# Preparing the first gated pairs late in layer A's attention, gate weights in half tiles, and output stores issued by ScalarE

## The chip, the cores and the metric

The kernel runs on one core of one Trainium2 chip. The metric is the device time of one execution in microseconds (us). TensorE is called PE here (PEld its weight loads), VectorE DVE, ScalarE ACT, GpSimd POOL, and SyncE, which in the kernel before issues all the DMAs, SP.

## The reference

A decoder trunk of two layers over 2048 tokens of width 1024. Layer A, the one that the change is in, is attention with a forget gate, 16 heads of 64, followed by a gate and an output projection:

```python
u = rmsnorm(h, norm_a_g[i])
q, k, v, f_logit, gate = jnp.split(u @ w_in_a[i], ...)
q, k = rmsnorm(q, qnorm_a_g[i]), rmsnorm(k, knorm_a_g[i])      # per head
log_f = jax.nn.log_sigmoid(f_logit + b_forget[i])
o = fox_attention(q, k, v, log_f)      # causal softmax(q k / 8 + c_q - c_k) v, c = cumsum(log_f)
h = h + (o * jax.nn.silu(gate)) @ w_out_a[i]
```

Layer B computes one shared K/V from the result, then attends in a window of 128 with a sink per head, gates and projects likewise. All in float32.

## The kernel before, in words

Layer A's attention is written as one loop, `for n, (u, p) in enumerate(steps)` (L1116). A unit `u` is a head and a chunk of 512 queries (64 units); a step is one pair of key blocks of a unit, 20 steps per head, 320 in all. A step takes about 2.7 us on the chip, from about 598 to 1474 us of the span.

In a step, `scores` multiplies keys by queries into score banks of PSUM (L975, L976, the mask L979; the tag "sc" has three places), ACT takes the exponential (L984; in a unit's last step L988) and rounds it to a high part (L989), POOL subtracts to get the low part (L990), and DVE adds the exponential to the running sum (L1001). `values` multiplies values by both parts three steps later (L1016); in a unit's last step it copies the result (L1024, ACT) and stores its halves to DRAM as `om` and `oc` (L1026, L1027, SP). Ahead of the scores, `max_pieces` computes row maxima for later units: products on PE (L927), a masked maximum on DVE (L938, L943), with one PSUM place "mx" between them, so that PE's next piece waits until DVE has read the one before.

Into the gaps goes the filler `gate()`: 768 products of the gate projection (L1050), twelve per weight tile of 512 KB (L1046, two places of the tag "wr"), 24 per output tile. When a tile is full, DVE scales it (L1057), ACT applies Tanh (L1058), DVE completes the SiLU (L1059), and SP stores it as `gt` (L1060). 720 of the products are fed in the loop, 48 remain for after it, the last two tiles.

After the loop comes `out_a`, the output projection (product L1219). Its left operand comes in "pairs" of 128 rows by 512 tokens (class `Pairs`, object `op`). A pair is loaded by `gated_load` (om L1167, oc L1168, gt L1169, and rd, the reciprocal sums, in two halves L1172) and prepared by `gated`: om + oc (L1182, POOL), times rd (L1183, DVE), times gt (L1184, DVE), rounded (L1185, ACT), low part (L1186, DVE). `PREP_AT = (284, 298)` loads and prepares pairs 0 and 1 inside the loop at these steps; pair 2 is loaded after it. The output weights of `out_a` are loaded by L122 and split by L131 (ACT) and L132 (DVE).

Python's order is not the chip's: a scheduler orders the instructions of each engine by its own costs, so what is written at step 284 may stand earlier on an engine. Each engine, SP too, then runs its instructions strictly in that order. A tile tag has a fixed number of places (`SLOTS`, L58); a new tile waits until all reads of the one whose place it takes are done.

Of the kernel before, what the change touches and what calls it, by code (L numbers as in the profile page):

```python
# [4 lines left out]

# [1 line left out]

# [15 lines left out]
P = 128  # L23
# [18 lines left out]
SUM_LAG = 5  # L42
LOAD_AT = 7

PREP_AT = (284, 298)

RAW_AT = 302

# [48 lines left out]
class Pairs:  # L97
# [6 lines left out]
        self.loaded = self.ready = 0  # L104

    def load(self, s, tags=("wh", "wl", "wh", "wl")):
        self.tiles[s] = [self.t.sb(tag, [P, CH]) for tag in tags]
        self.t.gated_load(s // NDT, s % NDT, self.tiles[s])
        self.loaded = s + 1

    def prepare(self, s):
        if s % 4 == 0:
            self.Y[s // 4] = self.t.sb("big", [P, 4, 2, CH], F32R)
        self.t.gated(self.y(s), self.tiles.pop(s))
        self.ready = s + 1

    def y(self, s):
# [28 lines left out]
class Trunk:  # L146
# [693 lines left out]
    def attention_a(self, op):  # L840
# [165 lines left out]
        def values(item):  # L1006
            u, p, ph, pl = item
            h, ch = units[u]
            v = heads[h][4]
            if p == 0:  # L1010
                state[u][1] = self.ps("pa", [P, CH])
            pv = state[u][1]
            last = p == 2 * ch + 1
            for n_, (k, q0, w, off) in enumerate(blocks(ch, p)):
                for i, src in enumerate((ph, pl)):
                    nc.tensor.matmul(  # L1016
                        pv[:, q0 : q0 + w], v[:, k, :], src[:, off : off + w],
                        start=(p == 0 and n_ == 0 and i == 0),
                        stop=(last and n_ == 1 and i == 1),
                    )  # L1020
            if last:
                state.pop(u)
                ov = self.sb("sq", [P, CH])
                nc.scalar.copy(ov, pv)  # L1024
                rows, cols = slice(h * HD, (h + 1) * HD), slice(ch * CH, (ch + 1) * CH)
                nc.sync.dma_start(out=d["om"][rows, cols], in_=ov[:HD, :])  # L1026
                nc.sync.dma_start(out=d["oc"][rows, cols], in_=ov[HD:, :])  # L1027

        def gate():


            for ch in range(NCH):
                rows, us = self.factor_rows(0, ch), []
                for dt in range(NDT):
                    us.append([self.sb(t, [P, CH], F32R) for t in ("wh", "wl")])
                    for k in range(2):
                        nc.sync.dma_start(out=f_(us[dt][k]), in_=d["ut"][ch, k, dt])
                for ft in range(NDT):
                    if gate_bank == "mx":
                        ps = self.ps("mx", [P, 2, CH])[:, 0]  # L1040
                    else:
                        ps = self.ps(gate_bank, [P, CH])
                    for dt in range(NDT):
                        if dt % 4 == 0:
                            w = self.sb(next(weight_slots), [P, 2, 2, 2, P], F32R)
                            nc.sync.dma_start(  # L1046
                                out=f_(w), in_=d["wg"][ft, :, dt // 2 : dt // 2 + 2]
                            )
                        for i, (wk, uk) in enumerate(((0, 0), (0, 1), (1, 0))):
                            nc.tensor.matmul(  # L1050
                                ps, w[:, dt // 2 % 2, wk, dt % 2, :], us[dt][uk],
                                start=(dt == 0 and i == 0), stop=(dt == NDT - 1 and i == 2),
                            )
                            if dt < NDT - 1 or i < 2:
                                yield
                    g = self.sb("sq", [P, CH])
                    nc.vector.tensor_tensor(g, ps, rows, ALU.mult)  # L1057
                    nc.scalar.activation(g, g, AF.Tanh, scale=0.5)  # L1058
                    nc.vector.scalar_tensor_tensor(g, g, 1.0, ps, ALU.add, ALU.mult)  # L1059
                    nc.sync.dma_start(  # L1060
                        out=d["gt"][ft * P : (ft + 1) * P, ch * CH : (ch + 1) * CH], in_=g
                    )
                    yield

        pieces, done, loaded = [], 0, 0

# [28 lines left out]
        yield  # L1095
        pht, plt = self.sb("big", [P, 4, 1024], F32R), self.sb("big", [P, 4, 1024], F32R)
        filler, fed, total = gate(), 0, NCH * NDT * NDT * 3
        gate_bank, weight_slots, rest = "pb", cycle(["wr"]), False

        def feed(n, pause=False):  # L1100

# [14 lines left out]
        for n, (u, p) in enumerate(steps):  # L1116
# [17 lines left out]
            if n == RAW_AT:  # L1134
                raw = self.sb("big", [P, NDT // 2, D])
                for p in range(NDT // 2):
                    op.weight_load(p, raw[:, p])
            if n in PREP_AT:
                op.load(PREP_AT.index(n), ("qn", "wh", "qn", "wl"))
                op.prepare(PREP_AT.index(n))  # L1140
        op.load(2, ("qn", "wh", "qn", "wl"))
        gate_bank, weight_slots = "mx", cycle(["st", "wr"])
        for item in pending:
            values(item)
            feed(fed + NDT)
# [2 lines left out]
            recips(*args)  # L1148
        for p in range(PAIRS_READY):
            op.weight_split(p)  # L1150
        for _ in filler:
            pass

# [20 lines left out]
                in_=d["rd"][h : h + 1, cols].to_broadcast([HD, CH]),  # L1174
            )

    def gated(self, y, tiles):

        nc = self.nc
        m, c, g, rb = tiles  # L1180
        yh, yl = (y[:, k] for k in range(2))
        nc.gpsimd.tensor_tensor(m, m, c, ALU.add)  # L1182
        nc.vector.tensor_tensor(m, m, rb, ALU.mult)  # L1183
        nc.vector.tensor_tensor(m, m, g, ALU.mult)  # L1184
        nc.scalar.copy(yh, m)  # L1185
# [350 lines left out]
```

## Time and profile before

| | us |
|---|---|
| median of 3 runs (lowest, highest) | 2511.03 (2509.34, 2516.57) |
| the profiled execution | 2511.7 |
| its span | 2509.9 |
| PE busy in the span | 2462.7 (98%) |
| DVE busy | 1760.2 (70%) |
| ACT busy | 1345.7 (54%) |
| POOL busy | 940.3 (37%) |

The shares are means over stages with different limits. Layer A's attention is the stretch from about 596 to 1494 us; PE is busy almost without a break in it. To read the profile for this change one goes to that stretch, looks at what PE waited for, and then at the timelines of the engines that PE waited for.

### The profile page before, as it was taken

What the parts mean: (1) busy time and instruction counts of PE and PEld (TensorE: products, weight loads), DVE (VectorE), ACT (ScalarE), POOL (GpSimd) and SP (SyncE); (2) the same over time, 40 slices, a digit from 0 to 9 for tenths busy, and PEclk for the clock granted to TensorE, in tenths of its full rate; (3) what the DMA queues carried; (4) which work ended last, traced back from release to release, by engine and by line L of the source; (5) the groups of instructions that cost most, each with busy time, mean ns of one, the idle gap of its engine ahead of it and who ended that gap; (6) DMA issues with size and microseconds to landing.
All of it is one profiled execution on the core that took longest, in us unless ns stands there. A gap on an engine that the chain in (4) does not pass through costs nothing. (4 is left out here: it accounts for less than half of the span.)

```text
span 2509.9 us, 37394 instructions
## 1 busy us (share of the span) xinstructions
PE 2462.7 (98%) x12320; PEld 2054.1 (82%) x12320; DVE 1760.2 (70%) x4255; ACT 1345.7 (54%) x2574; POOL 940.3 (37%) x611
## 2 busy tenths in 40 slices
PE   8999999999999999999999999999999999899999
PEld 6788899988878878877877778888888888688887
DVE  7656666736888888888888865556666323788885
ACT  5423333415777777877777651145332214777774
POOL 0000000014777777777777752200011000455542
PEclk9999999999999999999999999999999999999999
DMA  5656655787555745465475459955443424755551
GB/s 184 201 158 190 178 148 149 204 263 224 138 153 138 210 136 160 139 198 158 121 206 159 145 173 296 283 209 162 115 132 84 137 94 141 205 166 158 160 144 64
DMA packets 351521, 419.31 MB, mean 167 GB/s; under 512 B 64928, under 2 KB 248256, under 8 KB 345152
## 3 DMA queue, kind: packets, MB, share of 16 engines
q1 hardware_dynamic: 351328, 416.92, 56.7%
q8 instruction: 98, 1.61, 0.3%
q14 instruction: 95, 0.78, 0.1%
HBM read 265.29 MB, written 151.40 MB: 166 GB/s over the span
## 5 line engine op out<-in xcount | busy, mean ns | idle before, releaser
L750 PE MATMUL b<-wh,big 128*128 128x512 f32 (+3 forms) x2560 | 769.9, 375 | 9.4 <-ACT wh L480 9.3
L990 POOL TENSOR_TENSOR big<-st,big 128x1024 fp32r<-128x1024 f32 (+1 forms) x320 | 678.6, 2132 | 263.6 <-ACT big L989 181.2
L750 PEld LDWEIGHTS b<-wh,big 128*128 128x128 f32 x2560 | 471.4, 188 | 79.7 <-ACT wh L480 11.2
L750 PE MATMUL b<-wl,big 128*128 128x512 f32 (+3 forms) x1280 | 473.6, 370 | 1.2 <-DVE wl L481 1.2
L1001 DVE TENSOR_TENSOR ac<-ac,st 128x512 f32<-128x512 f32 (+3 forms) x576 | 354.7, 616 | 60.8 <-ACT ac L993 20.7
L984 ACT ACTIVATE st<-sc 128x512 f32<-128x512 f32 (+1 forms) x512 | 275.7, 585 | 130.6 <-PE sc L976 76.0
L1016 PE MATMUL pa<-big 128*128 128x512 f32 (+2 forms) x1280 | 332.5, 373 | 2.1 <-POOL big L990 1.2
L989 ACT CAST big<-st 128x1024 fp32r<-128x1024 f32 (+1 forms) x320 | 302.2, 945 | 7.8
L750 PEld LDWEIGHTS b<-wl,big 128*128 128x128 f32 x1280 | 241.4, 189 | 37.7 <-DVE wl L481 5.3
L1016 PEld LDWEIGHTS pa<-big 128*128 128x128 f32 x1280 | 224.5, 190 | 42.3 <-ACT sq L1024 8.1
L975 PE MATMUL sc<-big 128*128 128x512 f32 (+2 forms) x640 | 246.5, 385 | 1.3 <-DVE st L536 1.0
L938 DVE CUSTOM_DVE_ANT_0 mx<-mx,rot 128x128 f32<-128x128 f32 (+3 forms) x240 | 210.8, 878 | 48.0 <-PE mx L927 45.8
L489 ACT ACTIVATE sq<-b,r 128x512 f32<-128x512 f32 (+2 forms) x128 | 77.8, 608 | 302.8 <-PE b L750 299.8
L976 PE MATMUL sc<-big 67*128 67x512 f32 (+2 forms) x640 | 236.2, 369 | 0.0
L927 PE MATMUL mx<-big 66*128 66x128 f32 (+3 forms) x660 | 189.2, 360 | 6.3 <-DVE mt L938 3.2
L1050 PE MATMUL pb<-wh,wr 128*128 128x512 f32 x488 | 179.7, 399 | 6.3 <-DMA wr<-wg 6.0
L491 DVE TENSOR_REDUCE sm<-sq 128x8 f32<-128x512 f32 (+2 forms) x128 | 74.9, 585 | 139.5 <-ACT sq L489 139.3
L1307 POOL TENSOR_TENSOR st<-st,rs 128x1024 f32<-128x1024 f32 (+1 forms) x64 | 118.4, 1850 | 110.3 <-DVE rs L1306 102.1
L715 PE MATMUL b<-big,wh 128*128 128x512 f32 x512 | 158.5, 391 | 0.5 <-DVE st L721 0.5
L850 POOL MEMSET rot<- 128x1024 bf16 x1 | 1.0, 952 | 421.2 <-PE pb L343 421.2
L927 PEld LDWEIGHTS mx<-big 66*128 66x128 f32 x660 | 116.0, 192 | 35.6 <-DVE mt L938 8.3
L975 PEld LDWEIGHTS sc<-big 128*128 128x128 f32 x640 | 122.9, 192 | 21.6 <-ACT st L984 1.7
(251 smaller groups left out, 4348.3 us busy)
## 6 DMA issues: line engine op xcount, KB each, us to landing
wr<-wg SPq DMA_DIRECT2D x62, 512.0 KB, 4.7
va<-st SPq DMA_DIRECT2D x32, 512.0 KB, 4.6
ka<-st SPq DMA_DIRECT2D x64, 256.0 KB, 3.9
ut<-big SPq DMA_DIRECT2D x16, 1024.0 KB, 5.7
big<-ka SPq DMA_DIRECT2D x16, 1024.0 KB, 4.9
big<-qa SPq DMA_DIRECT2D x16, 1024.0 KB, 5.8
qb<-st SPq DMA_DIRECT2D x64, 256.0 KB, 3.9
big<-qb SPq DMA_DIRECT2D x16, 1024.0 KB, 7.7
```

Of the source, the lines that this page charges most:

```text
L715: nc.tensor.matmul(ps, W[k][dt][:, ft * P : (ft + 1) * P], u[ch][:, dt, :], start=(dt == 0 and i == 0), stop=(dt == NDT - 1 and i == 2),)
L750: nc.tensor.matmul(ps[:, :n], u[tb // 4][:, dt, us], W[k][dt], start=(dt == 0 and i == 0), stop=(dt == NDT - 1 and i == 2),)
L927: mm = nc.tensor.matmul(ps[:, b, :wb], qb[:66, i * P : (i + 1) * P], kb[:66, k0 + b * wb : k0 + (b + 1) * wb], start=True, stop=True,)
L938: nc.vector.tensor_tensor_reduce(out=lg, in0=lg, in1=mask, scale=1.0, scalar=NEG, op0=ALU.add, op1=ALU.max, accum_out=f_(o),)
L975: nc.tensor.matmul(o, ka[:, ks], qa[:, qs], start=not (last and n_), stop=False)
L976: nc.tensor.matmul(o, kb[:, ks], qb[:, qs], start=False, stop=not diag)
L984: nc.scalar.activation(pf[:, off : off + w], ps[:, :w], AF.Exp, scale=HD**-0.5)
L989: nc.scalar.copy(ph[:, :tw], pf[:, :tw])
L990: nc.gpsimd.tensor_tensor(pl[:, :tw], pf[:, :tw], f_(ph[:, :tw]), ALU.subtract)
L1001: nc.vector.tensor_tensor(a_, a_, pf[:, off : off + w], ALU.add)
L1016: nc.tensor.matmul(pv[:, q0 : q0 + w], v[:, k, :], src[:, off : off + w], start=(p == 0 and n_ == 0 and i == 0), stop=(last and n_ == 1 an ...
L1050: nc.tensor.matmul(ps, w[:, dt // 2 % 2, wk, dt % 2, :], us[dt][uk], start=(dt == 0 and i == 0), stop=(dt == NDT - 1 and i == 2),)
```

## The change

It has three parts. The core of the diff:

```diff
-PREP_AT = (284, 298)
+PAIR_AT = (298, 309)
 class Pairs:
     def load(self, s, tags=("wh", "wl", "wh", "wl")):
-        self.tiles[s] = [self.t.sb(tag, [P, CH]) for tag in tags]
+        if len(tags) == 4:
+            self.tiles[s] = [self.t.sb(tag, [P, CH]) for tag in tags]
+        else:
+            both = [self.t.sb(tag, [P, 2, CH]) for tag in tags]
+            self.tiles[s] = [t[:, k] for t in both for k in range(2)]
...
-    def prepare(self, s):
+    def prepare(self, s, adder=None):
...
-        self.t.gated(self.y(s), self.tiles.pop(s))
+        self.t.gated(self.y(s), self.tiles.pop(s), adder or self.t.nc.gpsimd)
...
-                nc.sync.dma_start(out=d["om"][rows, cols], in_=ov[:HD, :])
-                nc.sync.dma_start(out=d["oc"][rows, cols], in_=ov[HD:, :])
+                nc.scalar.dma_start(out=d["om"][rows, cols], in_=ov[:HD, :])
+                nc.scalar.dma_start(out=d["oc"][rows, cols], in_=ov[HD:, :])
...
-                        if dt % 4 == 0:
-                            w = self.sb(next(weight_slots), [P, 2, 2, 2, P], F32R)
-                            nc.sync.dma_start(
-                                out=f_(w), in_=d["wg"][ft, :, dt // 2 : dt // 2 + 2]
-                            )
+                        if dt % 2 == 0:
+                            w = next(weight_slots)
+                            nc.sync.dma_start(out=f_(w), in_=d["wg"][ft, :, dt // 2])
...
+        def weight_halves(*tags):
+            tiles = [self.sb(t, [P, 2, 2, 2, P], F32R) for t in tags for _ in range(2)]
+            return cycle([t[:, k] for t in tiles for k in range(2)])
...
-        gate_bank, weight_slots, rest = "pb", cycle(["wr"]), False
+        gate_bank, weight_slots, rest = "pb", weight_halves("wr"), False
...
-            if n in PREP_AT:
-                op.load(PREP_AT.index(n), ("qn", "wh", "qn", "wl"))
-                op.prepare(PREP_AT.index(n))
+            if n == PAIR_AT[0]:
+                op.load(0, ("qn", "wh", "qn", "wl"))
+            if n == PAIR_AT[1]:
+                op.prepare(0, nc.vector)
+        gate_bank, weight_slots = "mx", cycle(
+            list(islice(weight_halves("st"), 4)) + list(islice(weight_slots, 4))
+        )
+        op.load(1, ("st", "st"))
         op.load(2, ("qn", "wh", "qn", "wl"))
-        gate_bank, weight_slots = "mx", cycle(["st", "wr"])
...
             op.weight_split(p)
+        op.prepare(1, nc.vector)
         for _ in filler:
             pass
...
-        nc.gpsimd.tensor_tensor(m, m, c, ALU.add)
+        adder.tensor_tensor(m, m, c, ALU.add)
```

Pair 0 is written later in the loop and its addition goes to DVE; pair 1 goes behind the loop, with two places of the tag "st" instead of four others, its addition on DVE too. A gate weight tile of twelve products is loaded as two of six, into four places instead of two. The stores of a unit's output are issued by ACT. In the changed kernel the lines are numbered anew: the pair's addition is L1195, its products L1196 and L1197, its low part L1199, its loads L1180 (om), L1181 (oc), L1182 (gt), L1185 (rd); the gate tile's finish L1060 to L1062 and its store L1063, gate weights L1051, maxima L943 and L948, the sums L1006, the output weights' load and split L127, L136 and L137.

The first place is DVE's order between the last maxima (`m`, `mt`) and the running sums (`ac`), where a pair's products (`qn`) stand. Before, pair 0's two products (L1183, L1184):

```order
L938 ISA mx,mt<-mx,rot 128x2x288
L938 ISA mt 128x1
L1001 TENSOR_TENSOR ac<-ac,st 128x512
L1183 TENSOR_TENSOR qn<-qn,wl 128x512
L1001 TENSOR_TENSOR ac<-ac,st 128x512
L943 TENSOR_REDUCE mt<-mx 128x1
L1001 TENSOR_TENSOR ac<-ac,st 128x512
L1184 TENSOR_TENSOR qn<-qn 128x512
```

Now, pair 0's second product (L1197; its first stands four rows above it) and behind it the first product of pair 2 (L1196), which has the same places of "qn":

```order
L1197 TENSOR_TENSOR qn<-qn 128x512
L1006 TENSOR_TENSOR ac<-ac,st 128x512
L943 ISA mx,m<-mx,rot 128x2x384
L943 ISA m 128x1
L1006 TENSOR_TENSOR ac<-ac,st 128x512
L1006 TENSOR_TENSOR ac<-ac,st 128x384
L943 ISA mx,m<-mx,rot 128x2x448
L943 ISA m 128x1
L1006 TENSOR_TENSOR ac<-ac,st 128x256
L1196 TENSOR_TENSOR qn<-qn,wl 128x512
L1006 TENSOR_TENSOR ac<-ac,st 128x128
L943 ISA mx,m<-mx,rot 128x1024
```

Pair 0's products now stand in steps 268 and 269, before in 274 and 275; pair 2's first product, before in step 295, stands between the two sums of step 271, ahead of that step's maximum. On POOL, the additions (L1182 before, L1195 now) stand between the low parts. Before:

```order
L990 TENSOR_TENSOR big<-st,big 128x1024 x2
L1182 TENSOR_TENSOR qn<-qn,wh 128x512
L990 TENSOR_TENSOR big<-st,big 128x1024 x3
L1182 TENSOR_TENSOR qn<-qn,wh 128x512
L990 TENSOR_TENSOR big<-st,big 128x1024
```

Now, where the `qn` row is pair 2 and the `wh` row pair 3:

```order
L995 TENSOR_TENSOR big<-st,big 128x512
L1195 TENSOR_TENSOR qn<-qn,wh 128x512
L995 TENSOR_TENSOR big<-st,big 128x1024 x2
L1195 TENSOR_TENSOR wh<-wh,wl 128x512
L995 TENSOR_TENSOR big<-st,big 128x1024 x4
L995 TENSOR_TENSOR big<-st,big 128x896
```

Before, these were pairs 0 and 1, behind steps 273 and 276; pairs 2 and 3 came behind 294 and 296. Now pair 2 stands behind step 271 and pair 3 behind 273, and pair 0's addition has left POOL.

The second place is DVE's end of the loop, from the last running sum to the last gate tile. Before (L1057 and L1059 finish the gate tiles, L1183 to L1186 prepare pairs 3 and 4):

```order
L1059 SCALAR_TENSOR_TENSOR sq<-sq,pb 128x512
L132 TENSOR_TENSOR big<-big 128x1024 x2
L1057 TENSOR_TENSOR sq<-mx,rows 128x512
L902 TENSOR_TENSOR sq<-sc,ro_5213 48x32
L903 RECIPROCAL sq<-sq 48x32
L1059 SCALAR_TENSOR_TENSOR sq<-sq,mx 128x512
L1184 TENSOR_TENSOR wh<-wh 128x512
L1057 TENSOR_TENSOR sq<-pb,rows 128x512
L1186 TENSOR_TENSOR big<-wh,big 128x512
L1059 SCALAR_TENSOR_TENSOR sq<-sq,pb 128x512
L1183 TENSOR_TENSOR wh<-wh,wl 128x512
```

Now (L1060 and L1062 finish the gate tiles; the row L1196 is pair 4's):

```order
L1199 TENSOR_TENSOR big<-st,big 128x512
L1197 TENSOR_TENSOR wh<-wh 128x512
L1060 TENSOR_TENSOR sq<-mx,rows 128x512
L907 TENSOR_TENSOR sq<-sc,ro_5213 48x32
L1199 TENSOR_TENSOR big<-wh,big 128x512
L1062 SCALAR_TENSOR_TENSOR sq<-sq,mx 128x512
L908 RECIPROCAL sq<-sq 48x32
L1196 TENSOR_TENSOR wh<-wh,wl 128x512
L1197 TENSOR_TENSOR wh<-wh 128x512
L1060 TENSOR_TENSOR sq<-pb,rows 128x512
L1199 TENSOR_TENSOR big<-wh,big 128x512
L1062 SCALAR_TENSOR_TENSOR sq<-sq,pb 128x512
```

The last gate tile (`pb`) has moved behind pair 4's two products; before, it stood ahead of them. SP's queue there, now, from the loads of pair 1 (`st`) to those of pair 4 (`wl<-rd`):

```order
L1180 DMA st<-om 128x512
L1181 DMA st<-oc 128x512
L1182 DMA st<-gt 128x512
L1185 DMA st<-rd 64x512
L1063 DMA gt<-sq 128x512
L1185 DMA st<-rd 64x512
L1051 DMA st<-wg 128x512 x4
L127 DMA st<-in_w_out_a 128x1024
L1182 DMA wh<-gt 128x512
L1180 DMA wh<-om 128x512
L1182 DMA wh<-gt 128x512
L1185 DMA wl<-rd 64x512 x2
```

A store of a gate tile stands between the two halves of pair 1's rd; the load of w_out_a and those of pairs 3 and 4 stand behind them.

## Rows read from the trace of the kernel before

**Rows 1.** Busy time by stretch. Columns: the stretch, its length, busy us (and instructions) of PE, PEld, DVE, ACT and POOL, the granted TensorE clock, the share of the DMA engines, GB/s.

```profile
640.00:1300.00 660.00, 655.73 (x3216) 527.12 (x3216) 567.50 (x1058) 508.83 (x793) 510.23 (x242) 1.00 0.56 160
1300.00:1350.00 50.00, 45.14 (x222) 36.00 (x221) 41.24 (x74) 35.04 (x55) 35.51 (x18) 1.00 0.59 171
...
1400.00:1420.00 20.00, 16.76 (x69) 13.21 (x68) 17.49 (x25) 12.80 (x20) 16.27 (x8) 0.83 0.38 106
...
1470.00:1494.00 24.00, 21.15 (x97) 16.54 (x96) 15.90 (x20) 8.65 (x13) 7.61 (x5) 1.00 0.77 233
1494.00:1640.00 146.00, 146.00 (x646) 120.90 (x645) 77.07 (x104) 21.74 (x33) 34.60 (x26) 1.00 0.97 292
```

**Rows 2.** What PE waited for between 596 and 1494 us. Columns: PE's line, what ended the wait, us in total, times, the longest.

```profile
PE pb L1050 <- DMA wr<-wg: 6.0, 6, 1.8
PE mx L927 <- DVE mt L938: 3.2, 1, 3.2
PE mx L927 <- DVE mt L943: 3.0, 1, 3.0
PE b L1219 <- DVE sq L1059: 1.6, 1, 1.6
PE pa L1016 <- POOL big L990: 1.2, 1, 1.2
```

**Rows 3.** Timeline of PE, around 1349 and around 1412. Columns: start and duration in us, engine, line, operation, tiles, and in brackets the idle time before it with what ended it.

```profile
1349.54 0.56 PE L927 MATMUL mx<-big 66*128 66x320 f32 x2 [3.04 <-DVE mt L943]
...
1412.51 0.96 PE L927 MATMUL mx<-big 66*128 66x352 f32 x2 [3.24 <-DVE mt L938]
```

**Rows 4.** Busy time in the 8 us behind each of these two (columns as in rows 1).

```profile
1349.50:1357.50 8.00, 7.96 (x31) 6.43 (x32) 6.44 (x12) 4.66 (x7) 5.58 (x4) 0.79 0.32 81
1412.50:1420.50 8.00, 7.99 (x26) 6.33 (x27) 6.60 (x10) 4.08 (x6) 4.41 (x3) 0.64 0.17 61
```

**Rows 5.** Timeline of DVE, around 1345 and around 1408.

```profile
1345.31 2.85 DVE L1183 TENSOR_TENSOR qn<-qn,wl 128x512 f32<-128x512 f32 x1 [1.45 <-POOL qn L1182]
...
1408.22 2.84 DVE L1183 TENSOR_TENSOR qn<-qn,wl 128x512 f32<-128x512 f32 x1 [1.61 <-POOL qn L1182]
```

**Rows 6.** Line L1183 as a whole: durations in ns (shortest, median, longest), first and last start, forms.

```profile
L1183 DVE TENSOR_TENSOR wh<-wh,wl x29: 679/692/755, 1427.7 to 1642.2; 128x512 f32<-128x512 f32 x29
L1183 DVE TENSOR_TENSOR qn<-qn,wl x3: 680/2841/2848, 1345.3 to 1408.2; 128x512 f32<-128x512 f32 x3
```

**Rows 7.** Timeline of POOL, around 1408.

```profile
1406.89 1.29 POOL L1182 TENSOR_TENSOR qn<-qn,wh 128x512 f32<-128x512 f32 x1
1408.14 5.13 POOL L990 TENSOR_TENSOR big<-st,big 128x1024 fp32r<-128x1024 f32 x2
```

**Rows 8.** DMA issues on the page: tiles, queue, count, KB each, median us from issue to landing.

```profile
wr<-wg SPq DMA_DIRECT2D x62, 512.0 KB, 4.7
```

**Rows 9.** What SP's queue waited for between 590 and 1490 us (columns as in rows 2).

```profile
SPq L1026 <- ACT st L984: 110.7, 34, 6.6
```

**Rows 10.** Line L1168, the load of oc for a pair: issue to landing.

```profile
DMA to landing us min/median/max: 2.8/6.6/8.8
```

**Rows 11.** Timeline of PE at the loop's end: out_a's first and second tile.

```profile
1487.90 1.52 PE L1219 MATMUL b<-big 128*128 128x512 f32 x6
1491.03 2.35 PE L1219 MATMUL b<-big 128*128 128x512 f32 x9 [1.60 <-DVE sq L1059]
```

**Rows 12.** Timeline of DVE at the loop's end.

```profile
1477.73 0.64 DVE L1059 SCALAR_TENSOR_TENSOR sq<-sq,pb 128x512 f32<-128x512 f32 x1
...
1490.30 0.68 DVE L1059 SCALAR_TENSOR_TENSOR sq<-sq,pb 128x512 f32<-128x512 f32 x1
```

**Rows 13.** Timeline of SP's issues at the loop's end.

```profile
1478.40 0.32 SPq L1060 DMA_DIRECT2D gt<-sq  x1
1479.31 0.54 SPq L122 DMA_DIRECT2D st<-in_w_out_a  x1
...
1485.73 1.12 SPq L1172 DMA_DIRECT2D wl<-rd  x2
```

**Rows 14.** Line L1172, the loads of rd for a pair: issue to landing.

```profile
DMA to landing us min/median/max: 5.5/6.6/7.4
```

**Rows 15.** Timeline of ACT, around 830 and at the loop's end.

```profile
829.45 0.58 ACT L1024 COPY sq<-pa 128x512 f32<-128x512 f32 x1
829.91 1.07 ACT L989 CAST big<-st 128x1024 fp32r<-128x1024 f32 x1
830.86 1.59 ACT L984 ACTIVATE st<-sc 128x512 f32<-128x512 f32 x3
...
1488.88 0.63 ACT L1058 ACTIVATE sq<-sq 128x512 f32<-128x512 f32 x1 [0.41 <-DVE sq L1057]
```

**Rows 16.** Lines L1026 and L1027, the stores of a unit's output: durations of the issue in ns (shortest, median, longest), first and last start.

```profile
L1026 SPq DMA_DIRECT2D om<-sq x64: 445/472/1869, 605.6 to 1477.4; - x64
L1027 SPq DMA_DIRECT2D oc<-sq x64: 445/592/829, 606.2 to 1478.8; - x64
```

**Rows 17.** Timeline of PE, around 832.

```profile
831.88 0.33 PE L975 MATMUL sc<-big 128*128 128x384 f32 x1
```

**Rows 18.** The page's groups of instructions: busy us, mean ns, and idle time before them with what ended most of it.

```profile
L984 ACT ACTIVATE st<-sc 128x512 f32<-128x512 f32 (+1 forms) x512 | 275.7, 585 | 130.6 <-PE sc L976 76.0
...
L975 PE MATMUL sc<-big 128*128 128x512 f32 (+2 forms) x640 | 246.5, 385 | 1.3 <-DVE st L536 1.0
```

More of the change, by code (lines that the diff above doesn't have):

```diff
@@ L3 @@
 from functools import partial
-from itertools import cycle
+from itertools import cycle, islice
 import numpy as np
@@ L1043, in gate @@
                     for dt in range(NDT):
-                        if dt % 4 == 0:
-                            w = self.sb(next(weight_slots), [P, 2, 2, 2, P], F32R)
-                            nc.sync.dma_start(
-                                out=f_(w), in_=d["wg"][ft, :, dt // 2 : dt // 2 + 2]
-                            )
+                        if dt % 2 == 0:
+                            w = next(weight_slots)
+                            nc.sync.dma_start(out=f_(w), in_=d["wg"][ft, :, dt // 2])
                         for i, (wk, uk) in enumerate(((0, 0), (0, 1), (1, 0))):
                             nc.tensor.matmul(
-                                ps, w[:, dt // 2 % 2, wk, dt % 2, :], us[dt][uk],
+                                ps, w[:, wk, dt % 2, :], us[dt][uk],
                                 start=(dt == 0 and i == 0), stop=(dt == NDT - 1 and i == 2),
@@ L1175, in gated_load, with gated @@
             )
-    def gated(self, y, tiles):
+    def gated(self, y, tiles, adder):
         nc = self.nc
```

## The prediction, made before the changed kernel ran

> **What bounds the kernel now.** I read the busy time by stretch first. In layer A's attention TensorE is the bound: 655.73 of 660.00 us busy in 640 to 1300 [rows 1]. VectorE has 86% there, ScalarE 77%, so they cost only where TensorE must wait. The table of what TensorE waited for is therefore nearly the whole list of what can be won [rows 2]: 6.0 us for gate weights in six waits, 3.2 and 3.0 us for maxima, 1.6 us at the end for VectorE's sixth gate tile, 1.2 us for POOL. TensorE's timeline puts the two long waits at 1349.5 and 1412.5 [rows 3], and the clock shows a second price: in the 8 us after them the granted clock is 0.79 and 0.64 of full speed, a mix of the 2.4 and the 1.2 GHz level [rows 4], while stretches with short waits (1.6 us at 1491 among them) keep 1.00 [rows 1]. I price that as 8 x 0.21 = 1.7 us and 8 x 0.36 = 2.9 us.
>
> **Why TensorE waited there.** VectorE's timeline has the same event twice [rows 5]: the product L1183 of a prepared pair waited 1.45 or 1.61 us for POOL's addition, and then took 2.85 us, though the same form takes 0.69 us elsewhere [rows 6]. POOL was in its low part L990 then [rows 7]. So VectorE was 1.45 + 2.16 = 3.6 us late, and TensorE idle 3.0 us: lateness less about 0.55 us. The Trainium skill (SBUF — State Buffer, "Who interferes with whom") says that a VectorE instruction with two SBUF inputs and a POOL instruction that reads SBUF need one port pair, which the first holds to its end; the 2.84 beside 0.69 us agrees. By that page alone every such operation beside a busy POOL is held; of the three here, one took 0.68 us.
>
> **The change, term by term** (against the profiled execution).
>
> *(a) Gate weights: -5.5 us.* Loads of six products into four places let a load be issued 18 products before its use, not 12. The loop spreads 720 products over 320 steps, so that is 8 steps against 5. Landing took 4.7 us for 512 KB [rows 8]. SP also loses 128 stores, for one kind of which it waited 110.7 us in all, with the weights' loads queued behind [rows 9]. It gets some 64 more loads. Bounds: 0 (other queues on SP still late) and -6.0; I take nearly all, since cover grows by half and the head of the queue goes.
>
> *(b) The two old stalls: -10.8 us.* 3.04 + 3.24 idle, 1.7 + 2.9 of clock. Those operations are no longer at those places. Bounds: 0 and -10.8 (what returns is in c).
>
> *(c) The pairs' new places: +7.3 us.* The order shows that the change doesn't simply put pair 0 behind the last maxima: its addition now stands on VectorE at step 258 and its products at 268 and 269; the later half only is behind. Pair 2's addition moves some 23 steps up on POOL, and its L1196 stands on VectorE at step 271, ahead of a maximum that TensorE waits for. Its load of om needs the place that pair 0's L1197 at step 269 still reads. Two steps are 5.5 us. From that product: 0.7 (itself), 0.4 (an issue), landing 2.8 to 6.6 (the row of this load's neighbour, [rows 10]), 1.3 for the addition: 5.2 to 9.0 us. So VectorE waits 0 to 3.5, I take 2.0; with the hold of 2.15 and less 0.5 TensorE idles 3.6 us, and the clock costs the mean of the two old ones, 2.3. Pair 3's product at step 275 has the same chain with more room: +0.6. The early two-input operations beside POOL: a lone hold of 2.15 us, less the same 0.55, would idle TensorE 1.6 us, and I give it half a chance to happen once: +0.8. Bounds of (c): +1 (all landed) to +12 (two full stalls). By the page above, all four early operations held would make it about +10.
>
> *(d) The end: +7.7 us.* Before, out_a's second tile waited only 1.60 us, to 1491.03, for the gate tile that VectorE finished at 1490.98 [rows 11, 12]. Now that tile stands on VectorE behind pair 4's L1196 and L1197, so behind its loads. On SP these come after a chain: the gate store (its tile ready near 1478.4 by [rows 12]), the second half of pair 1's rd, landing 4.5 later (2.8 to 6.6), VectorE's two products (1.3), SP's w_out_a load (0.5 [rows 13]), which waits for that place, and behind it gt, om, rd. Pair 4's second rd half is so issued near 1487.0; rd took 5.5 at least, 6.6 in the middle [rows 14]; at +5.8 it lands at 1492.8. Two products, the gate tile's L1060, ScalarE's Tanh (0.63 us, [rows 15]) and L1062 (3.4 us in all) give 1496.2: 5.2 us later than now. A wait of that length follows the rule of [rows 4], so +2.5 of clock. Bounds: +1 (short landings) and +13 (6.6 twice, full clock loss).
>
> *(e) ScalarE issues the stores: +6 us.* 64 pairs of issues at 0.47 and 0.59 us [rows 16] are 68 us on an engine with 23% to spare. Whether it reaches TensorE hangs on the score banks: three in turn, each rewritten after its exponential. In the example the exponential that starts at 830.86 ends its first part at 831.39, and the product that rewrites its bank starts at 831.88 [rows 15, 17]: 0.49 us of slack, just behind a unit's copy L1024, where the stores will stand. I took that slack for all 576 tiles (512 exponentials L984 and 64 of L988, each against the score product that next writes its bank, [rows 18]), held ScalarE 1.06 us behind each of 64 copies, let idle time absorb it, and added the largest excess of each cluster: 7.2 us at nine places. At 0.8 us held it is 4.0, at 1.6 us 21. I take 6, since SP's shortest issue is 0.445 us [rows 16] (0.89 the pair). Bounds: 0 (ScalarE's issue costs nothing) and 35 (2 us held).
>
> SP's remaining work, and the 1.2 us for POOL, I leave as they are: they lie beside TensorE's work.
>
> **Sum:** -5.5 - 10.8 + 7.3 + 7.7 + 6.0 = +4.7 us. The profiled execution took 2511.7 us, 0.7 above the median of three runs (2511.03), so 2516.4 against it and **2515.7 us** against the median. A measurement here tells 0.3% (7.5 us) from no change, so this counts as the same, though on the slow side.
>
> **Rivals.**
> *Slower: ScalarE becomes the late engine.* Place: between a unit's copy and its next exponentials, 64 times. Two engines now issue DMAs at once, and the longest store issue in the trace is 1.87 us [rows 16]. Decides from 1.25 us held per pair (11 us by the count above). At 1.6 us the term is 21 instead of 6: **2531 us**. Against it: most issues are at 0.45 to 0.6. The Trainium skill (Perfetto Trace Analysis, "DMA Instruction — HWDGE") has an issuing sequencer held from the lock of the one descriptor generator to the end of its work; issue rows here last 0.32 to 0.6 us, which agrees, but no run shows two issuers at once. A second page (DMA: Bandwidth & Descriptors, "Issuing engines are not separate DMA queues") calls what moves to the other engine small; by it the term would be near 0 and the time 2509.7 us, inside the forecast's case. Chance 0.22.
> *Faster: stalls go and don't come back.* The loads land by the short ends of [rows 10, 14], pair 4's chain costs 2 and the early pairs 2, ScalarE's issues 1.5: -5.5 - 10.8 + 2 + 2 + 1.5, **2500 us**. For it: the landing's short end is 2.8 us, and VectorE has 14% to spare. Chance 0.25.
> *The end alone goes worse.* Two rd landings of 6.6 and a clock loss over several us give +13 in (d): **2521 us**. Chance 0.08.
> *The change does not do what it says.* The order already says so for pair 0; if in addition the weights' waits stay, (a) is 0: **2521 us**. In the chance of the forecast.
>
> **How the numbers follow.** Forecast 0.45, slower rivals 0.30, faster 0.25. Same is within 2503.5 and 2518.6. Range: 2500 takes in most of the faster case, 2528 the lower half of the slow one; some 2 in 10 stay outside.
>
> **What would show it.** TensorE's waits for gate weights under 1 us (a); no maxima wait near 1412 and clock 1.00 there (b); in place of that at 1349 one of 2 to 4 us three steps earlier (near 1342), behind an L1196 of 2.8 us (c); out_a's second tile near 1496 with L1062 before it (d); ScalarE's store rows at 0.45 to 0.6 us and several short waits of TensorE for an exponential (e). A stretch 640 to 1300 without new waits on ScalarE would prove (e) wrong; a second tile of out_a before 1492 would prove (d) wrong.

## The result and the profile after

In seven runs of each, the changed kernel took 2530.13 us (2522.6 to 2533.35) and the kernel before 2516.62 us (2509.34 to 2519.73): a ratio of 1.0048, interval 1.0034 to 1.0063, or 12 us slower. The forecast had 4.7 us and an upper end of 2528. The first three runs of before, on which the forecast was set, were also 5.6 us below its median of seven. The profiled execution has a span of 2528.4 us, 18.5 longer than that of before, which lay at the fast end of its kernel's runs; so the profile is read for places and for what a wait cost in this one execution; what an edit is worth comes from ratios.

What PE waited for between 596 and 1520 us, after (columns as in [rows 2], which it answers to):

```profile
PE pa L1021 <- POOL big L995: 5.9, 6, 1.8
PE b L1232 <- DVE sq L1062: 4.5, 1, 4.5
PE mx L932 <- DVE m L943: 4.3, 3, 3.4
PE sc L980 <- DVE sq L907: 2.5, 2, 1.3
PE pb L1053 <- DMA wr<-wg: 2.4, 2, 1.9
PE mx L932 <- DVE mt L943: 2.3, 2, 1.7
```

Gate weights fell from 6.0 to 2.4 us. The waits for maxima are still there (4.3 and 2.3), and three kinds are new or larger: values waiting for POOL (1.2 before), out_a's second tile (1.6 before), and score banks behind DVE's L907.

Busy time by stretch, after, and below the last "..." four stretches of 8 us around or behind a wait (columns as in [rows 1]):

```profile
640.00:1300.00 660.00, 653.08 (x3207) 526.40 (x3206) 566.61 (x1057) 505.45 (x793) 506.31 (x241) 1.00 0.58 161
...
1400.00:1420.00 20.00, 20.00 (x96) 16.36 (x96) 17.98 (x32) 16.70 (x26) 17.82 (x9) 1.00 0.40 111
...
1306.00:1314.00 8.00, 7.22 (x29) 6.15 (x30) 6.34 (x14) 2.69 (x5) 3.66 (x3) 0.79 0.42 89
1349.30:1357.30 8.00, 8.00 (x27) 6.83 (x28) 4.88 (x9) 4.28 (x7) 4.40 (x3) 0.62 0.27 72
1477.80:1485.80 8.00, 7.10 (x21) 5.24 (x22) 6.84 (x9) 2.35 (x4) 2.20 (x1) 0.57 0.81 250
1500.00:1508.00 8.00, 7.85 (x24) 6.25 (x25) 3.37 (x6) 0.93 (x2) 1.28 (x1) 0.66 0.98 317
```

In 640 to 1300 PE lost 2.6 us against [rows 1] although the weights' waits became shorter. The stall of 1412 is gone (1400 to 1420 is busy throughout, at clock 1.00, against 0.83). In its place stand two drops of the clock at 1306 and 1349 (means of 0.79 and 0.62), and two more at the loop's end, to 0.57 and 0.66, where before had 1.00.

A second reading needs no single wait: the start of a step's first score product (L975, now L980), counted from that of step 0, less the same in before. It is where PE stands against before, in us (positive is late):

| step | 8 | 64 | 128 | 192 | 256 | 270 | 280 | 300 | 309 | 319 |
|---|---|---|---|---|---|---|---|---|---|---|
| changed kernel | 1.4 | 1.5 | 3.8 | 2.9 | 4.5 | 9.3 | 6.6 | 0.8 | 0.4 | 2.0 |
| late_pairs | 1.4 | 1.4 | 4.0 | 2.6 | 3.9 | 5.3 | -4.0 | -11.4 | -11.5 | -7.7 |
| half_tiles_alone | 0.0 | 0.0 | -0.5 | -3.3 | -1.6 | -2.0 | -4.3 | -1.9 | -0.6 | -0.1 |
| stores_on_act_alone | 1.4 | 1.3 | 4.5 | 6.1 | 6.3 | 8.6 | 0.2 | -1.1 | -1.4 | 0.1 |
| stores_back_on_sp | 0.0 | 0.0 | -0.5 | -2.9 | -0.8 | -1.7 | -2.6 | -9.2 | -2.4 | -2.4 |
| pairs_behind_loop_act | 1.4 | 1.3 | 3.4 | 2.0 | 3.6 | 5.0 | -4.4 | -11.7 | -11.9 | -8.4 |
| pairs_behind_loop_sp | 0.0 | -0.1 | -0.6 | -2.8 | -1.2 | -1.7 | -8.3 | -14.1 | -14.3 | -9.7 |

(The lower rows are kernels of the next section.) At step 309 the changed kernel stood level with before: what it had won it had also lost. Then the end: out_a's first tile started 6.1 us later than in [rows 11], its second 9.1, and its last product 15.9 (1680.5 against 1664.6 us). The last 2.6 us of the 18.5 fall behind out_a, in code that the change does not touch, and are not explained.

PE, around two waits for maxima and at the end:

```profile
1306.78 0.65 PE L932 MATMUL mx<-big 66*128 66x416 f32 x2 [1.73 <-DVE mt L943]
...
1349.29 0.85 PE L932 MATMUL mx<-big 66*128 66x288 f32 x2 [3.38 <-DVE m L943]
...
1477.84 1.36 PE L1021 MATMUL pa<-big 128*128 128x512 f32 x4 [1.83 <-POOL big L995]
1480.05 1.01 PE L1021 MATMUL pa<-big 128*128 128x256 f32 x3 [0.86 <-POOL big L995]
...
1492.69 0.39 PE L1053 MATMUL mx<-wh,st 128*128 128x512 f32 x1
...
1493.82 0.39 PE L1053 MATMUL pb<-wh,wr 128*128 128x512 f32 x1
...
1500.15 5.49 PE L1232 MATMUL b<-big 128*128 128x512 f32 x12 [4.49 <-DVE sq L1062]
```

DVE at the same places:

```profile
1304.30 1.03 DVE L1195 TENSOR_TENSOR qn<-qn,wh 128x512 f32<-128x512 f32 x1 [1.82 <-DMA wh<-oc]
...
1344.99 2.84 DVE L1196 TENSOR_TENSOR qn<-qn,wl 128x512 f32<-128x512 f32 x1 [1.53 <-POOL qn L1195]
...
1493.11 0.69 DVE L1060 TENSOR_TENSOR sq<-mx,rows 128x512 f32<-128x512 f32 x1 [0.96 <-PE mx L1053]
1493.72 0.17 DVE L907 TENSOR_TENSOR sq<-sc,ro 48x32 f32<-48x32 f32 x1
...
1498.02 0.69 DVE L1060 TENSOR_TENSOR sq<-pb,rows 128x512 f32<-128x512 f32 x1 [1.07 <-DMA gt<-sq]
```

At 1306 PE waited for a maximum that stood behind L1195, pair 0's addition on DVE, which itself waited 1.82 us for the load of oc. At 1349 the maximum stood behind pair 2's product L1196: 1.53 us of waiting for POOL and 2.84 us of work, the event of [rows 5] once more. At the end there are two events. In the loop's last steps PE waited 1.83 and 0.86 us for POOL's low parts, where before had one such wait of 1.25 us, and the clock fell to 0.57 over the next 8 us. Then the last gate tile: its first operation on DVE (L1060 at 1498.02) waited for neither pair 4 nor PE, but for a store of a gate tile (gt<-sq). The tag sq has two places, and both were taken: one by the gate tile of 1493.11, whose store was still running, the other by the reciprocals of the last sums (L907 at 1493.72).

### The profile page after: what moved, and what is told of

Same layout as the page of the kernel before. It is cut to its first block, busy times and chain, and to the rows that moved or that the text cites. A ratio compares the mean times of both kernels' runs of the same rounds, so it can differ in the third digit from the quotient of the medians.

```text
span 2528.4 us, 37514 instructions
## 1 busy us (share of the span) xinstructions
PE 2471.4 (98%) x12320; PEld 2060.9 (82%) x12320; DVE 1765.2 (70%) x4257; ACT 1342.4 (53%) x2574; POOL 936.7 (37%) x609
## 5 line engine op out<-in xcount | busy, mean ns | idle before, releaser
L1006 DVE TENSOR_TENSOR ac<-ac,st 128x512 f32<-128x512 f32 (+3 forms) x576 | 355.6, 617 | 46.1 <-ACT ac L998 19.3
L989 ACT ACTIVATE st<-sc 128x512 f32<-128x512 f32 (+1 forms) x512 | 282.5, 583 | 140.2 <-PE sc L981 63.4
L943 DVE CUSTOM_DVE_ANT_0 mx<-mx,rot 128x128 f32<-128x128 f32 (+3 forms) x240 | 210.6, 877 | 61.2 <-PE mx L932 56.9
L980 PE MATMUL sc<-big 128*128 128x512 f32 (+2 forms) x640 | 245.4, 384 | 3.7 <-DVE sq L907 2.5
L1053 PE MATMUL pb<-wh,wr 128*128 128x512 f32 x496 | 186.3, 403 | 2.6 <-DMA wr<-wg 2.4
L1232 PE MATMUL b<-big 128*128 128x512 f32 x576 | 140.7, 398 | 6.5 <-DVE sq L1062 4.5
```

What stands on the lines that cost most here:

```text
L943: nc.vector.tensor_tensor_reduce(out=lg, in0=lg, in1=mask, scale=1.0, scalar=NEG, op0=ALU.add, op1=ALU.max, accum_out=f_(o),)
L980: nc.tensor.matmul(o, ka[:, ks], qa[:, qs], start=not (last and n_), stop=False)
L989: nc.scalar.activation(pf[:, off : off + w], ps[:, :w], AF.Exp, scale=HD**-0.5)
L1006: nc.vector.tensor_tensor(a_, a_, pf[:, off : off + w], ALU.add)
L1053: nc.tensor.matmul(ps, w[:, wk, dt % 2, :], us[dt][uk], start=(dt == 0 and i == 0), stop=(dt == NDT - 1 and i == 2),)
```

## The experiments

Ten kernels ran, each timed in five rounds against before on the same chip. stores_on_act_alone and half_tiles_alone edit the kernel before, all others the changed one. The changed kernel was not timed again in these rounds, so a gain "below the changed kernel" is a difference of two ratios to before. The readings of places come from one profiled execution of each kernel. In the edits "..." stands for lines left out, and the comments behind # are added here.

**Pairs 0, 2 and 3 behind the last maxima.** Every DVE and POOL instruction of these pairs is queued behind the running sum and the low part of step 309 (the last maximum stands at step 306):

```diff
-        self.t.gated(self.y(s), self.tiles.pop(s), adder or self.t.nc.gpsimd)
+        with ExitStack() as held:
+            if s <= PAIRS_READY + 1:
+                for ins in self.behind:      # the sum and the low part of step 309
+                    held.enter_context(self.t.tc.issue_after(ins))
+            self.t.gated(self.y(s), self.tiles.pop(s), adder or self.t.nc.gpsimd)
...
```

> The changed kernel with the DVE and POOL work of pairs 0, 2 and 3 queued behind the running sum and the low part of step 309, so behind the last maxima. Theory A (the pairs' early places and the end of the loop are the loss, the stores a few us): the waits of 1.7, 0.6, 0.3, 3.4 and 0.5 us for maxima between 1306 and 1365 go, with their clock of some 4 us; about 10 us below the changed kernel, 1.001 of the kernel before. Rival B (ACT's stores are the loss, by late casts and POOL): these stay, and the gain is under 4 us, 1.003 to 1.004 of before.

Measured: 2515.29 us, ratio 0.9992 (0.9983 to 1.0000); against the changed kernel's 1.0048 that is 14 us. PE's waits, 590 to 1520 us:

```profile
PE pa L1027 <- POOL big L999: 6.1, 8, 1.7
PE b L1239 <- DVE sq L1068: 3.2, 1, 3.2
...
PE mx L936 <- DVE mt L952: 0.6, 2, 0.3
```

The long waits for maxima are gone (0.6 in all remain), and the table shows where: 4.5 us late at step 256 in the changed kernel, 9.3 at step 270; here it falls to -4.0 at step 280, when before has its first stall, and to -11.4 at step 300, after its second. The early places of the pairs cost 11.9 us by step 309. Theory A holds, with some 4 us more than it expected; rival B's bound of 4 us does not.

**The last two gate tiles, weights swapped.** In the changed kernel the first of the two takes the four halves of "st", which come late, so the scheduler ran 19 products of the second, then 24 of the first, then 5 of the second.

```diff
-            list(islice(weight_halves("st"), 4)) + list(islice(weight_slots, 4))
+            list(islice(weight_slots, 4)) + list(islice(weight_halves("st"), 4))
```

> The changed kernel with the weight places of the last two gate tiles swapped: the first takes the four halves of wr, the second those of st. PE then runs 24 products of the one and 24 of the other, where the changed kernel runs 19, 24 and 5 and completes both tiles within 1.4 us. Theory A (out_a's second tile waited because both tiles completed at once and the second needed a place of sq that the first one's store still read): out_a's second tile starts 4 to 7 us earlier, total 6 to 10 us below the changed kernel. Rival (the forecast's chain: pair 4's loads hold the tile): DVE has both tiles ahead of pair 4's product in this kernel too, so the same gain; the run pin_pair4 tells the two apart.

Measured: 2519.43 us, 1.0011 (1.0003 to 1.0020), 9 us below the changed kernel. out_a's second tile on PE:

```profile
1497.36 3.11 PE L1232 MATMUL b<-big 128*128 128x512 f32 x9 [1.89 <-DVE sq L1062]
```

It waited 1.89 us instead of 4.49 and started at 1497.36 instead of 1500.15, in an execution whose loop ran 3.6 us later (its wait at 1349 came at 1352.89). The last gate tile's L1060 (1495.23) has no wait for gt<-sq here. The gain is in the range of both theories, but only a part of it is that wait, because the swap did a second thing that neither theory named. The first tile's weights now lie in "wr" and are there early, so its products stand between the last values:

```profile
1479.10 0.40 PE L1053 MATMUL mx<-wh,wr 128*128 128x512 f32 x1
...
1480.92 1.30 PE L1021 MATMUL pa<-big 128*128 128x512 f32 x4
```

POOL's last three low parts are as late as without the swap: they start 3.5 us later, in a loop that runs 3.6 us later (the first row is the changed kernel, the second tail_swap):

```profile
1472.35 7.65 POOL L995 TENSOR_TENSOR big<-st,big 128x1024 fp32r<-128x1024 f32 x3 [0.22 <-ACT big L994]
```

```profile
1475.83 7.73 POOL L995 TENSOR_TENSOR big<-st,big 128x1024 fp32r<-128x1024 f32 x3 [0.20 <-ACT big L994]
```

PE does not wait for them any more, and the clock stays at 1.00 there. Against before, PE lost from the start of step 319 to out_a's first tile 4.3 us in the changed kernel and 0.8 here, from the first to the second tile 3.0 and 0.3, and within out_a 6.8 and 1.6.

**Pair 4 behind the last gate tile**, with PE's order as in the changed kernel:

```diff
+        if s == PAIRS_READY + 2:
+            with self.t.tc.issue_after(self.t.tile_done.ins):    # DVE's last L1062
+                return self.prepare_(s, adder)
...
```

> The changed kernel with pair 4's work on DVE queued behind the last gate tile's finish; PE's order stays 19, 24, 5. Forecast's chain (pair 4's loads hold the tile): out_a's second tile starts 4 to 5 us earlier. Theory A (place of sq): L1060 still waits for the store of the tile before, so the start moves by 0.5 to 1 us only, and the time is the changed kernel's within 2 us.

Measured: 2526.06 us, 1.0037 (1.0024 to 1.0050); this interval meets that of the changed kernel. DVE there:

```profile
1500.14 0.69 DVE L1066 TENSOR_TENSOR sq<-pb,rows 128x512 f32<-128x512 f32 x1 [2.94 <-DMA gt<-sq]
```

With pair 4 out of the way DVE simply stood idle for 2.94 us: the tile's L1066 still waited for the store of the tile before it to leave one of the two places of "sq", and PE waited 4.8 us. So pair 4's loads, the forecast's reason, did not hold the tile; the place did. Both tiles completed within 1.1 us (last products at 1492.69 and 1493.82 in the changed kernel), and the reciprocals of the last sums, made between them, held the second place.

**Both edits.**

> Both edits, pairs behind step 309 and swapped weight places. Theory A: the two gains add up, 16 to 20 us below the changed kernel, 0.996 to 0.999 of the kernel before, with what is left of ACT's stores (waits for POOL and for sq, 5 to 6 us) against the gate weights' waits of before (6 us). Rival B: no better than 1.001 of before.

Measured: 2510.94 us, 0.9977 (0.9968 to 0.9985): 18 us below the changed kernel, in theory A's range, but less than the 14 and 9 of each alone. Beside the late pairs the swap brings 4 us, and out_a's second tile still waits 2.9 us (3.2 without it), so the gate tile's wait is hardly what it saves here; where its gain lies was not followed. The product is already faster than before.

**The same, stores on SP again** (`nc.scalar.dma_start` back to `nc.sync.dma_start`).

> The version late_pairs_tail_swap with the outputs' stores issued by SP again; pairs 0, 2 and 3 stay behind step 309 and the weight places stay swapped. Theory A (stores on ACT cost some 4 us through waits of PE for POOL and for a score bank behind DVE's L911, against what SP gains): 2 to 5 us faster than that version, 0.996 of before, with no waits for DVE's L911 and fewer for POOL. Forecast's size (6 us): 6 us faster. Rival C (SP's queue is relieved and that is worth more): 2 to 6 us slower, with waits of PE for gate weights back above 3 us.

Measured: 2507.78 us, 0.9967 (0.9955 to 0.9979). Too near the one above to part by time. By step 309 PE stood 13.5 us ahead of before, where the version on ACT had 11.6, but by step 319 they had lost 8.2 and 3.6 us of it. POOL in this stretch:

```profile
1457.21 1.29 POOL L1202 TENSOR_TENSOR wh<-wh,wl 128x512 f32<-128x512 f32 x1 [3.82 <-DMA wl<-oc]
```

and the wait of PE that follows:

```profile
1460.86 1.28 PE L1027 MATMUL pa<-big 128*128 128x512 f32 x3 [2.60 <-POOL big L999]
```

POOL stood 3.82 us at pair 3's addition for its oc, and then ran six low parts without a gap.

**Stores on ACT alone**, in the kernel before:

> The kernel before with the outputs' stores issued by ACT, nothing else. The order shows what comes with it: pair 0's addition moves from behind step 273 to 258, its first product from 274 to 265, pair 1's from 279 to 271, ahead of the last maxima still. Theory A: the early places come from this part of the change, and the waits for maxima stay (3 us twice, with clock); with the stores' own 3 to 5 us the time is 1.001 to 1.004 of before. Rival C: SP relieved, 0.997 to 0.999.

Measured: 2519.23 us, 1.0015 (1.0004 to 1.0026), 4 us. PE's waits:

```profile
PE pa L1016 <- POOL big L990: 6.5, 7, 1.8
PE mx L927 <- DVE mt L943: 4.7, 5, 2.3
...
PE sc L975 <- ACT st L984: 0.8, 2, 0.5
```

By step 256, where no pair is prepared yet, PE was 6.3 us late. Waits for an exponential (the last row) make 0.8 us of it; those for POOL up to there 2.5, for maxima 1.8. Behind it the waits for maxima are 2.3 and 1.5 us, not 3 twice. Theory A's range holds, rival C's does not.

**Half tiles alone**, in the kernel before, on SP:

> The kernel before with gate weights in halves of six products, nothing else; pairs stand as before (274, 279, 293). Forecast: the waits for gate weights fall from 6.0 us to under 1, so 0.998 of before. Rival: SP still waits with the stores' turn, and the weights' waits stay at 4 to 6 us: 1.000.

Measured: 2513.16 us, 0.9987 (0.9975 to 0.9998), 3 us faster. PE's waits:

```profile
PE mx L927 <- DVE mt L943: 8.4, 4, 4.0
...
PE pb L1048 <- DMA wr<-wg: 2.0, 5, 0.7
```

6.0 us of waits for weights became 2.0, where the forecast had under 1; the waits for maxima came out 2 us longer in this execution. The interval just excludes no change.

**Stores back on SP**, in the changed kernel, nothing else:

> The changed kernel with the outputs' stores issued by SP, nothing else. The order shows pair 0's products at steps 278 and 279 instead of 268 and 269, pair 2's at 297 instead of 271, and PE's last two gate tiles as 7, 18, 3, 6 and 14 products. Theory A (the engine of the stores decided where the scheduler puts the pairs): pair 2's wait of 3.4 us goes, pair 0's stays in part; 8 to 12 us below the changed kernel, 1.000 to 1.002 of before. Rival B (ACT's issues by themselves are the loss): the gain is the same, but in the stretch 640 to 1300, not in 1300 to 1370.

Measured: 2516.55 us, 0.9998 (0.9985 to 1.0010), 12.5 us below the changed kernel. The table tells where. Nothing is lost by step 256 (-0.8 us against 4.5), which is 5.3 us, in rival B's stretch. Between steps 256 and 309 the edit wins nothing: two waits for maxima, 2.25 us at 1347 and 3.35 at 1428, with the clock at 0.57 and 0.58 behind them, stand in place of those of 1306 to 1365, and at step 309 the lead over the changed kernel is down to 2.8 us. In this execution the rest comes behind step 309, where PE waits 1.24 us for POOL and not 2.7; out_a's second tile waits as long as in the changed kernel (4.5 us). So the pairs did move, as theory A had it, but their new places are not where the gain lies. The edit was worth 2.5 and 6 us where the pairs were held in place, and 12.5 here; why so much more at the loop's end was not separated.

**Pairs 2 and 3 behind the loop, pair 0 behind step 306**, with swapped weights and half tiles, once with the stores on SP and once on ACT. The pairs stand at the same steps in both:

```diff
-PAIR_AT = (298, 309)
+PAIR_AT = (290, 306)
...
+        op.behind = self.summed.ins, self.lowered.ins     # now those of step 319
         op.load(1, ("st", "st"))
```

> The version late_tail_stores_on_sp with pair 0 behind step 306 instead of 309, and the additions and products of pairs 2 and 3 behind the loop's last step. In late_tail_stores_on_sp PE stood 13.5 us ahead of before by step 309 and only 5.3 by step 319, with waits of 0.9, 1.2 and 2.6 us behind pair 2's and 3's work on DVE and POOL in steps 312 to 316. Theory A: most of these 8 us stay won, so 4 to 8 us below that version, 0.994 to 0.995 of before. Rival: pairs 2 and 3 are then late for out_a (each 5.5 us of products), which gives the time back as waits in out_a's first chunk: 0.9965 to 0.998 of before.

> The same with the outputs' stores issued by ACT, as in the changed kernel; the pairs stand at the same steps in both (306 to 308, and behind the loop), so the two differ by the stores' engine and by what the scheduler makes of it in PE's order. Forecast's term: 6 us slower than the version on SP, with waits for exponentials. Theory A: 3 to 6 us slower by PE's waits for POOL (0.6 and 0.8 us near 609 and 620) and for DVE's L911 (1 to 1.4 us twice), with few waits for exponentials. Rival C (SP relieved): faster than the version on SP.

Measured on SP: 2502.57 us, **0.9954** (0.9940 to 0.9967), faster than both kernels by 11 us or more; on ACT 2509.54 us, 0.9978 (0.9968 to 0.9988). The stores' engine, with the order that the scheduler makes of it, is thus worth 0.24%, 6 us (the two intervals just part). PE's waits on SP, and then on ACT:

```profile
PE sc L984 <- ACT st L993: 2.8, 1, 2.8
PE pb L1059 <- DMA wr<-wg: 2.4, 7, 0.5
```

```profile
PE pa L1027 <- POOL big L999: 2.5, 4, 0.8
PE sc L984 <- DVE sq L911: 2.4, 2, 1.5
...
PE sc L984 <- ACT st L993: 1.0, 2, 0.8
```

On ACT 2.5 us for POOL and 2.4 for L911, as theory A had it, and 1.0 for exponentials; on SP neither of the first two stands in the list. Its one wait for an exponential, 2.8 us, lies at 1438, where ACT had stood 3.10 us at pair 0's rounding (L1206), not at a store. The step from late_tail_stores_on_sp, 0.9967 to 0.9954, is 3 us with intervals that overlap. Pairs 2 and 3 were not late for out_a: PE has no wait in its first chunk but the second tile's 1.1 us.

## Why the prediction was wrong

The step that failed most is (d), the end of the loop: 7.7 us in the forecast, 15.7 measured, for another reason than the forecast's, and with a term for POOL that the forecast left as it was. (c) was short by 4.6 us. Against the profiled execution of before the terms up to step 309 had -3.0 us, and PE stood at +0.4 there. By its steps:

*(a) Gate weights, -5.5.* Smaller: 3.6 us of waits in the changed kernel, 4.0 and a ratio of 0.9987 alone. A third of the waits or more stays although a load can now be issued 18 products ahead; what holds it was not tried.

*(b) The old stalls, -10.8.* Held in size: with nothing put in their place (late_pairs) PE gained 7.9 us from step 256 to 280 and 7.4 more to step 300, waits of before for weights of 1.81 and 1.35 us among them.

*(c) The pairs' new places, +7.3.* Measured 11.9 by step 309, near the upper bound of 12. The mechanism at step 271 was as forecast: DVE waited 1.53 us (2.0 forecast), was held at 2.84, PE idled 3.38 (3.6). The term that was missing is pair 0's addition on DVE at step 258. I counted it only as a two-input operation beside POOL; it is also the first to need pair 0's oc, and waited 1.82 us for it, which cost PE 1.73 us and 8 x 0.21 = 1.7 of clock. Second, the clock behind 1349 was 0.62, so 3.0 us and not 2.3. With these, 7.3 + 3.4 + 0.7 = 11.4.

*(d) The end, +7.7.* The step that failed. It put the last gate tile behind pair 4's loads. The order said so, and pair 4's L1196 did run at 1495.53, without waiting; what the tile waited for was a place of sq, and pin_pair4 shows that without pair 4 PE waits as long (4.8 us). I had read DVE's and SP's order there and not PE's, where 19, 24 and 5 products put two tiles to an end at once, with two places for them and for the reciprocals of the last sums. This wait cost 2.9 us more than in before, and 8 x 0.34 = 2.7 of clock: not far from the 5.2 and 2.5 of the forecast, but by luck, since its chain did not occur.

What made the end twice as long is not in the forecast's sum. It left POOL's 1.2 us of waits as they were. They became 5.9 us in all, 2.7 of them at 1477.84 and 1480.05, and the clock behind them was 0.50 from 1478.2 to 1485.0, in which PE was busy 5.9 us: 3.0 us of it are the clock's. tail_swap shows that it need not be so: POOL is as late there, and PE has gate products to run meanwhile. And out_a had a further wait of 1.99 us for DVE's L1243 at 1634, with some 1.7 us of clock behind it; it is 0.7 us in pin_pair4, absent in tail_swap, and its cause stays open. From step 309 to out_a's end PE lost 15.7 us.

*(e) The stores, +6.* Near in size and wrong in its reason. By step 256 the changed kernel is 5.3 us behind stores_back_on_sp; by time the stores' engine was worth 2.5 us (not clear of noise), 4 and 6 in the other pairs of kernels. I held ACT 1.06 us behind each copy and let it reach PE through the score banks; the sign that I gave for it, short waits for exponentials, is not among the changed kernel's waits. ACT, around the copy's stores in the changed kernel (ACTq are the issues):

```profile
605.27 0.98 ACT L994 CAST big<-st 128x896 fp32r<-128x896 f32 x1
605.44 0.49 ACTq L1031 DMA_DIRECT2D om<-sq  x1
605.97 0.60 ACTq L1032 DMA_DIRECT2D oc<-sq  x1
606.67 0.60 ACT L993 ACTIVATE st<-sc 128x512 f32<-128x512 f32 x1 [0.42 <-PE sc L981]
```

The issues run beside the cast that stands ahead of them, and the next exponential starts 0.42 us late, not 1.06. In 62 of the 64 pairs of stores the first was issued while another instruction of ACT ran, and in 48 ACT then stood idle 0.7 us or less. What changed is PE's order. PE at the same place, after, and then before:

```profile
606.14 2.02 PE L1021 MATMUL pa<-big 128*128 128x512 f32 x8
...
608.12 0.40 PE L1021 MATMUL pa<-big 128*128 128x512 f32 x1
609.15 0.84 PE L1021 MATMUL pa<-big 128*128 128x512 f32 x3 [0.63 <-POOL big L995]
...
610.06 0.40 PE L980 MATMUL sc<-big 128*128 128x512 f32 x1
```

```profile
606.33 2.02 PE L1016 MATMUL pa<-big 128*128 128x512 f32 x8
608.18 0.39 PE L975 MATMUL sc<-big 128*128 128x512 f32 x1
...
609.24 0.98 PE L1016 MATMUL pa<-big 128*128 128x512 f32 x4
```

Before, the next scores (608.18) stand between the eighth and the ninth product of values; now twelve products of values stand ahead of them, the last three wait 0.63 us for POOL, and the scores start at 610.06. POOL runs without a gap up to 610 in both. The 0.6 us near 609 and the 0.8 us near 620 recur in every kernel here with the stores on ACT, and in none with them on SP. That the scheduler makes this of the stores' place is seen in the order; why it does so was not tried. By step 256 the waits for POOL make 2.0 us. The other 2.5 are two waits, at 774 and 1214, for a score bank that DVE's L907 frees; they occur in every kernel here that has both stores on ACT and half tiles, and in no other. L907 takes a place of sq, as the unit's output does, and in pairs_behind_loop_act (there L911) it waited 3.0 us in four waits for the store oc<-sq. In the changed kernel the profile puts its waits down to other engines, so there this is not shown.

**The rivals.** "ACT becomes the late engine" gave a time near the measured one, 2531 us, for a reason that did not occur: the issues took 0.45 and 0.61 us in the middle, and held ACT far less than the 1.6 us of that rival. That its time comes out right is luck. "The end alone goes worse" (+13) was the closest in its place, though not in its reason, two late landings of rd. The lines of the Trainium skill that I set beside terms fared thus: DVE's and POOL's shared port pair (SBUF — State Buffer, "Who interferes with whom") agrees again with 2.84 against 0.69 us, and pair 0's early products were held as well (1.75 and 1.47 us); that issuing from another engine saves only a sequencer's time, small beside the transfer (DMA: Bandwidth & Descriptors, "Issuing engines are not separate DMA queues"), agrees as far as the issue goes (0.42 us held in the rows above); the time went through the order.

## What to carry to other kernels

Where a scheduler places the work, an edit's first effect is the order that comes out of it: read the order of the bound engine too, not only that of the engines that the edit names, and hold moved work where it is meant to stand. Ask of every wait which resource ends last, among them the places of a tag that several results share when they complete together. A wait that is small before the change is not a constant: an order with less work between two products lets it through. A wait of the engine that sets the pace can cost its length and then, here, 1.7 to 3.0 us of clock.

## What the runs showed of the hardware

A DMA issue on ACT need not wait for the instruction ahead of it to finish: 0.17 us after the cast's start the first store was issued (605.44 against 605.27), so 1.09 us of issues cost 0.42 us. The issues' middle durations are close to those of SP in [rows 16], though 50 of the 128 overlap an issue on SP in time; one took 2.39 us, all others under 1 us:

```profile
L1031 ACTq DMA_DIRECT2D om<-sq x64: 452/453/490, 605.4 to 1481.7; - x64
L1032 ACTq DMA_DIRECT2D oc<-sq x64: 452/609/2394, 606.0 to 1482.2; - x64
```

Waits of PE of nearly the same length were followed by different clocks: 1.73 us at 1306 by 0.79, but 1.86 us for weights at 1070 by 1.00. In other kernels 2.3 us were followed by 0.79 (stores_on_act_alone, 1405) and by 0.57 (stores_back_on_sp, 1347), and 3.4 us by 0.62. I had priced the drop by the length of a wait; these rows do not bear that out, and what else decides stays open.
